# Four first products of two later pairs made ahead from a turned copy of x; the identity made on the chip; the first norm's weights as one row

## The chip, the cores and the metric

The kernel runs on one core of a Trainium2 chip. The metric is the device time of one execution in microseconds (us); of the kernel before there are three runs, and their median counts. A core has five engines, each with a queue of its own: PE (TensorE: matmuls, with the weight loads shown apart as PEld), DVE (VectorE), ACT (ScalarE), POOL (GpSimd) and SP (SyncE, which here issues nearly all DMA transfers). On-chip data lie in SBUF (128 partitions); PE writes to PSUM, eight banks of 128 x 512 floats, of which this kernel uses four with the tag `mm` and four with the tag `acc`.

## The reference

One decoder block on x of 1024 tokens x 1024 features, in float32:

```python
h = x + 0.5 * swiglu(rms_norm(x, ffn1_norm), ffn1_w1, ffn1_w3, ffn1_w2)
u = rms_norm(h, mix_norm)
...                      # u @ w_in, three groups of dilated attention, pooling, gates
h = h + merged @ w_out
h = h + 0.5 * swiglu(rms_norm(h, ffn2_norm), ffn2_w1, ffn2_w3, ffn2_w2)
return rms_norm(h, final_norm)

def rms_norm(x, g):      # per token
    return x * rsqrt(mean(x * x) + 1e-6) * g
def swiglu(x, w1, w3, w2):
    return (silu(x @ w1) * (x @ w3)) @ w2
```

The change touches only the first norm and the first two matrices of the first feed-forward part (D_FF is 2816).

## The kernel before

**Products in three parts.** Every float32 operand is split in a high part (rounded, type f32r) and a low part (the rest). A product of two operands is three matmuls: high x high, high x low, low x high. A *product* here is one of 512 x 512 of x by a 512 x 128 column block of weights, with 4 pieces of 128 along the sum: 12 matmuls of 128 x 128 by 128 x 512.

**Seven products for eight.** x is cut in two halves of features and two of tokens, a weight block in two halves of features and two neighbouring column blocks of 128. With sums and differences of the quarters, seven products give what eight would (Strassen's scheme in Winograd's form). `Quad` holds one such block of `w1` (A) or `w3` (B); `Pair` j (11 of them, `NPAIR`) is the quad A and the quad B of 256 columns. `ORDER = (1, 6, 2, 7, 5, 4, 3)` is the order of the seven products in a quad. Product 1 is x's first quarter `b11` (tokens 0 to 511, features 0 to 511) by the weight's quarter a11; product 2 is `b21` (same tokens, other features) by a12. Products 1 and 2 share one bank, and so do 5 and 3. `Quad.operand(m)` forms the weight side (DVE sums, then `split`: ACT writes the high part, POOL or every third time DVE the rest; four buffers `wc`). `a_out` and `b_out` take the results out of the banks: for product 1, a copy by ACT into `u2` (for A the upper half of the pair's first row y0, for B a tile u); 6 adds to `u2`; product 2's bank, which by then holds 1 + 2, gets its silu (A), or is multiplied into y0 (B).

**The order of work.** Pairs 0 to 2 are begun by `begin_up1` and by `Entry`, whose engine order is written out by hand; `up` finishes them and then runs pairs 3 to 10 one after the other. The results (seven sums a pair) go to DRAM by DMAs on SP; the weights come through `Stream` on SP, into seven buffers of the tag `raw`.

**The start (`begin_up1`).** SP loads the tiles of x (`load_rows`: 128 tokens x 1024 features) and the first weight blocks. For each of the first four tiles ACT squares and sums (`squares`, L274), DVE and POOL make the inverse root (`inverse`), DVE scales the lower 512 features in place by it and by the norm's weights (`scaled_part`, L285), PE turns the result by four transposes against `ident` (`Rows`, L407), ACT writes the high part of the turned tile (L408) and DVE the low part (L411). The first product, `entry.product(0)`, needs all four tiles. PE fills the time before with `keep_on(n)`, n matmuls of ones on ones into a bank `idle` that nobody reads. The norm's weights come as 128 x 8 numbers on ACT's queue, `ident` from DRAM on the same queue; DVE widens the weights to 128 x 1024 (`widen`) and PE turns them into a row that all partitions hold (`gains`). Behind the first product the upper 512 features follow in the same way, with `entry.product(1)` to `(3)` between them.

Of the kernel before, what the change touches and what calls it, by code (L numbers as in the profile page):

```python
# [10 lines left out]
F32 = mybir.dt.float32  # L11
F32R = mybir.dt.float32r
# [125 lines left out]
def tile_block(  # L138
# [46 lines left out]
    def row(name):  # L185
        return keep.tile([P, 1024], F32, tag="raw", bufs=RAW_BUFS, name=name)
# [2 lines left out]
        return keep.tile([P, D], F32, tag="h", bufs=NT, name=name)  # L189


    consts.tile([P, 24], F32, name="pad")
# [79 lines left out]
    def squares(t, out):  # L272
        inv[t] = small.tile([P, 2], F32, tag="nst", name=f"nst_{t}")
        ac.activation(out, h[t], AF.Square, accum_out=inv[t][:, 0:1])  # L274
# [31 lines left out]
    class Sevens:  # L306


        def __init__(self, name, X, fw, fs=None):
            self.name, self.X, self.fw, self.fs = name, X, fw, fs or fw  # L310
            self.n_lo = 0
            self.terms = (0, 1, 2)

        def half_tile(self, tag, n):
            return self.fs.tile([P, HALF], F32, tag=tag, bufs=4, name=f"{tag}_{self.name}{n}")
# [19 lines left out]
    class Quad:  # L335
# [49 lines left out]
        def run(self, m, back=True):  # L385
            if m not in self.w:
                self.operand(m)
            w, n = self.w.pop(m), self.n
            x = {1: "b11", 2: "b21", 3: "b22", 4: "t4", 5: "t1", 6: "t2", 7: "t3"}[m]
            key = {1: "x", 2: "x", 5: "v", 3: "v"}.get(m, m)  # L390
            if m not in (2, 3):
                self.bank[key] = bank("mm" if key in ("x", "v") else "acc", f"u_{self.sv.name}{n}{m}")
            self.sv.product(self.bank[key], w, x, start=m not in (2, 3))
            if m == 3 and back:
                raws.back(2)
            return self.bank[key]
# [140 lines left out]
    class Pair:  # L537
# [48 lines left out]
        def b_out(self, m, p):  # L586
            lows, highs = slice(0, HALF), slice(HALF, S)
            u, j = self.u, self.j
            if m == 1:
                u[2] = self.u2(f"{j}2")  # L590
                ac.activation(u[2], p, AF.Copy)
            elif m == 6:
                ve.tensor_tensor(u[2], p, u[2], op=OP.add)
            elif m == 2:
                c = self.place(0, lows)
                ve.tensor_tensor(c, p, c, op=OP.mult)
            elif m == 7:
                u[3] = self.sv.half_tile("u", f"{j}3")
                ve.tensor_tensor(u[3], p, u[2], op=OP.add)
            elif m == 5:  # L600
                c = self.sv.half_tile("u", f"{j}4")
                ve.tensor_tensor(c, p, u[3], op=OP.add)
                d = self.place(1, highs)
                ve.tensor_tensor(d, d, c, op=OP.mult)
            elif m == 4:
                ve.scalar_tensor_tensor(u[3], p, -1.0, u[3], op0=OP.mult, op1=OP.add)
                d = self.place(1, lows)
                ve.tensor_tensor(d, d, u[3], op=OP.mult)
            else:
                ve.tensor_tensor(u[2], p, u[2], op=OP.add)  # L610
                d = self.place(0, highs)
                ve.tensor_tensor(d, d, u[2], op=OP.mult)
# [31 lines left out]
    def up(sv, sums, between, name, room, begun):  # L644
# [30 lines left out]
            begun[-1].finish()  # L675
        for j in range(len(begun), NPAIR - 1):
            q, then = then or Pair(sv, j, sums), None
            for m in ORDER:
                q.a(m)
            if j == NPAIR - 2:  # L680
                between()
            for m in ORDER[:-2]:
# [5 lines left out]
            for m in ORDER[-2:]:  # L688
                q.b(m)
            q.finish()  # L690
        d = Down(name, sums, sv.half_tile, end)
# [180 lines left out]
    ac.activation(warm, mhalf, AF.Silu)  # L872

    scope = ExitStack()
# [5 lines left out]
    def load_rows(*ts):  # L880
        for t in ts:
            nc.sync.dma_start(h[t], x[t * P:(t + 1) * P, :])

    gain_row = keep.tile([P, D], F32, tag="gain", bufs=1, name="gain_ffn1")
    square = row("square")
    columns_tile = tmp("columns")
    columns = columns_tile.rearrange("p (k c) -> p k c", k=KT)

    def load_all():
        load_rows(0, 1, 2, 3)  # L890
        raws.depth = 2
        raws.load()
        load_rows(4)
        raws.depth = 3
        raws.load()
        load_rows(5)
        raws.depth = 4
        raws.load()
        load_rows(6, 7)
        raws.depth = 6  # L900
        raws.load()
# [5 lines left out]
    def begin_up1():  # L907
# [5 lines left out]
        def keep_on(n):  # L913

            for _ in range(n):
                pe.matmul(idle[:, :P], ones, ones, start=True, stop=True)

        def widen(b):
            k = slice(4 * b, 4 * b + 4)
            ve.tensor_copy(columns[:, k], gain1[:, k, None].to_broadcast([P, 4, P]))  # L920

        def gains(b):

            p = bank("acc", f"gain{b}")
            for k in range(4):
                pe.transpose(p[:, k * P:(k + 1) * P], columns[:, 4 * b + k], ident)
            return p

        r = {}
# [5 lines left out]
        keep_on(12)  # L935
        widen(0)
        squares(0, square)
        widen(1)
        inverse(0)
        g = [gains(b) for b in range(2)]  # L940
        keep_on(2)
        ve.tensor_copy(gain_row[:, LOWS], g[0])
        for t in range(1, 4):
            squares(t, square)
        inverse(1)
        rows(0, "b11", LOWS)
        keep_on(2)
        rows(1, "b11", LOWS)
        inverse(2)
        inverse(3)  # L950
        keep_on(2)
# [4 lines left out]
        rows(2, "b11", LOWS)  # L956
        keep_on(3)
        rows(3, "b11", LOWS, "mm")
        keep_on(2)
        ac.activation(gain_row[:, HIGHS], g[1], AF.Copy)  # L960
        for t in range(4):
            r[t].lower()
        sv1.terms = (0, 2, 1)
# [4 lines left out]
            r[t].keep(h[t][:, LOWS])  # L968

        square2 = columns_tile  # L970
        squares(4, square2)
        for t in (0, 1):
            rows(t, "b21", HIGHS)
        entry.product(1)
        entry.out(0)
        entry.operand(2)
# [2 lines left out]
        r[0].lower()  # L979
        for t in (2, 3):  # L980
            rows(t, "b21", HIGHS)
        for t in (1, 2):
            r[t].lower()
        entry.product(2)
        entry.out(1)
        squares(5, square2)
        r[3].lower()
        for t in range(4):
            r[t].keep(h[t][:, HIGHS])
        entry.product(3)  # L990
# [1357 lines left out]
```

## Time and profile before

| | us |
|---|---|
| median of 3 runs | 1892.95 (1892.79 to 1893.48) |
| the profiled execution | 1892.07 |
| its span in the trace | 1890.2 |
| PE busy | 1879.9 |
| DVE busy | 1331.9 |
| ACT busy | 772.8 |
| POOL busy | 712.2 |

The span is the stretch from the first to the last instruction in the trace; the execution's time holds some 1.9 us around it. All times in the trace count from the span's start. A busy PE is one with a matmul under way; matmuls overlap by about half, so their distance, not their duration, gives the pace.

### The profile page before, as it was taken

To read this page: it belongs to the slowest core of one execution; us is meant where nothing else is said; L and a number is where in the kernel's file an instruction comes from. 1 tells how busy PE (TensorE), PEld (TensorE's weight loads), DVE (VectorE), ACT (ScalarE), POOL (GpSimd) and SP (SyncE) were. 2 spreads that over 40 slices of the span, in tenths; PEclk is the share of its full clock that TensorE was granted. 3 is DMA by queue.
4 is the path that set the end of the run, shared out by engine and by line. 5 is a ranking of instruction groups with operands and counts; after the bars stand their busy time and mean duration, and the time that the engine had idled before them with its cause. 6 is when DMAs were issued, how large, how long until landed. Compare 5 with 4: busy or idle time off the path is not lost.

```text
span 1890.2 us, 24694 instructions
## 1 busy us (share of the span) xinstructions
PE 1879.9 (99%) x8822; PEld 1561.9 (83%) x8822; DVE 1331.9 (70%) x1975; ACT 772.8 (41%) x1394; POOL 712.2 (38%) x533
## 2 busy tenths in 40 slices
PE   9999999999999999999999999999999999999998
PEld 8888888888888888888888888888888888888887
DVE  6776556657786777557885896887665566577867
ACT  7323333333334553334445772363333323334344
POOL 5433333331223254444555357543333333312221
PEclk9999999999999999999999999999999999999999
DMA  5154223436566526765668968744332223454654
GB/s 191 60 198 166 84 89 106 139 111 216 170 224 210 183 84 210 236 219 188 224 236 314 322 224 289 270 153 149 140 127 103 84 102 118 137 189 162 226 197 145
DMA packets 144019, 330.79 MB, mean 175 GB/s; under 512 B 17560, under 2 KB 39064, under 8 KB 142360
## 3 DMA queue, kind: packets, MB, share of 16 engines
q1 hardware_dynamic: 140152, 318.36, 48.6%
q10 hardware_dynamic: 3744, 10.85, 1.6%
q8 instruction: 70, 1.15, 0.3%
q14 instruction: 53, 0.43, 0.1%
HBM read 229.61 MB, written 99.55 MB: 174 GB/s over the span
## 4 chain that ended last, share of the span: by engine, by line
PE 57%; DVE 2%; ACT 1%; DMA 1%; issue 0%; POOL 0%; ACTq 0%; DVEq 0%; SPq 0%
PE u_mixm L331 15%; PE d_f L815 11%; PE wo L2028 4%; PE yp L1770 1%; PE u_f20b L331 1%; PE u_f21a L331 1%; PE u_f210b L331 1%; PE u_f210a L331 1%; PE u_f29b L331 1%; PE u_f29a L331 1%; PE u_f28a L331 1%; PE u_f27b L331 1%; PE u_f27a L331 1%; PE u_f26b L331 1%; PE u_f26a L331 1%; PE u_f25b L331 1%
## 5 line engine op out<-in xcount | busy, mean ns | idle before, releaser
L815 PE MATMUL d_f<-bhi_f,ahi_f 128*128 128x512 f32 x616 | 240.2, 390 | 0.0
L815 PE MATMUL d_f<-bhi_f,alo_f 128*128 128x512 f32 x616 | 239.7, 389 | 0.0
L815 PE MATMUL d_f<-blo_f,ahi_f 128*128 128x512 f32 x616 | 239.6, 389 | 0.0
L772 POOL TENSOR_TENSOR alo_f<-g_f,ahi_f 128x512 fp32r<-128x512 f32 x60 | 85.9, 1448 | 270.0 <-ACT ahi_f L768 270.0
L331 PE MATMUL u_mixm<-xhi_t_mix,wc_mixm 128*128 128x512 f32 x608 | 157.3, 391 | 0.1
L815 PEld LDWEIGHTS d_f<-bhi_f,ahi_f 128*128 128x128 f32 x616 | 115.7, 188 | 24.2 <-ACT h L415 0.5
L815 PEld LDWEIGHTS d_f<-bhi_f,alo_f 128*128 128x128 f32 x616 | 115.6, 188 | 24.2
L815 PEld LDWEIGHTS d_f<-blo_f,ahi_f 128*128 128x128 f32 x616 | 115.7, 188 | 23.7
L331 PEld LDWEIGHTS u_mixm<-xhi_t_mix,wc_mixm 128*128 128x128 f32 x608 | 113.5, 188 | 23.9 <-ACT wc_mixm L319 0.7
L331 PE MATMUL u_mixm<-xhi_b_mix,wc_mixm 128*128 128x512 f32 x456 | 120.4, 391 | 0.0
L322 POOL TENSOR_TENSOR wc_mixm<-s_mixm,wc_mixm 128x512 fp32r<-128x512 f32 x52 | 76.6, 1475 | 104.9 <-ACT wc_mixm L319 94.0
L331 PEld LDWEIGHTS u_mixm<-xhi_b_mix,wc_mixm 128*128 128x128 f32 x456 | 84.9, 188 | 17.3
L319 ACT ACTIVATE wc_mixm<-s_mixm 128x512 fp32r<-128x512 f32 x76 | 47.0, 628 | 109.4 <-DVE s_mixm L373 54.6
L768 ACT ACTIVATE ahi_f<-g_f 128x1024 fp32r<-128x1024 f32 x84 | 81.9, 975 | 3.1 <-DMA g_f<-gs_f 2.0
L331 PE MATMUL u_mixm<-xlo_t_mix,wc_mixm 128*128 128x512 f32 x304 | 81.3, 389 | 0.0
L322 POOL TENSOR_TENSOR wc_mixm<-raw,wc_mixm 128x512 fp32r<-128x512 f32 x40 | 60.2, 1505 | 40.8 <-ACT wc_mixm L319 32.4
L2028 PE MATMUL wo<-w_o,o_hi 128*128 128x512 f32 x224 | 69.3, 390 | 0.0
L768 ACT ACTIVATE bhi_f<-s_f2w 128x512 fp32r<-128x512 f32 x55 | 33.0, 628 | 86.3 <-DVE s_f2w L790 67.6
L768 ACT ACTIVATE bhi_f<-s_f1w 128x512 fp32r<-128x512 f32 x55 | 33.1, 629 | 83.4 <-DVE s_f1w L790 70.2
L331 PEld LDWEIGHTS u_mixm<-xlo_t_mix,wc_mixm 128*128 128x128 f32 x304 | 57.1, 188 | 12.0
L772 DVE TENSOR_TENSOR alo_f<-g_f,ahi_f 128x1024 fp32r<-128x1024 f32 (+1 forms) x48 | 57.6, 1200 | 7.6 <-ACT ahi_f L768 7.5
L331 PE MATMUL u_mixm<-xlo_b_mix,wc_mixm 128*128 128x512 f32 x228 | 61.0, 389 | 0.0
(1332 smaller groups left out, 4751.9 us busy)
## 6 DMA issues: line engine op xcount, KB each, us to landing
g_f<-gs_f SPq DMA_DIRECT2D x70, 512.0 KB
gs_f<-y_f SPq DMA_DIRECT2D x88, 256.0 KB
raw<-in_w2a_dram SPq DMA_DIRECT2D x35, 512.0 KB
raw<-in_w2b_dram SPq DMA_DIRECT2D x35, 512.0 KB
gs_f<-gb_f SPq DMA_DIRECT2D x46, 256.0 KB
raw<-in_w1a_dram SPq DMA_DIRECT2D x22, 512.0 KB
raw<-in_w3a_dram SPq DMA_DIRECT2D x22, 512.0 KB
raw<-in_w1b_dram SPq DMA_DIRECT2D x22, 512.0 KB
```

The costliest lines, as they stand in the source:

```text
L319: ac.activation(w[:, 0], src, AF.Copy)
L322: eng.tensor_tensor(w[:, 1], src, w[:, 0].bitcast(F32), op=OP.subtract)
L331: pe.matmul(p, a, b, start=(start and n == 0), stop=(n == 11), skip_group_check=not start)
L768: ac.activation(hi[:, c], src, AF.Copy)
L772: eng.tensor_tensor(lo[:, d], src[:, o], hi[:, d].bitcast(F32), op=OP.subtract)
L815: pe.matmul(self.banks[m][t], l, r, start=(first and q == 0), stop=(last and q == 2))
L1770: pe.matmul(p, a, b, start=(j == 0), stop=(j == 11))
L2028: pe.matmul(banks[m][t], l, r, start=(st == 0 and j == 0 and q == 0), stop=(st == 1 and j == 1 and q == 2))
```

## The change

1. `ident` is made by POOL (`affine_select` on the tile of ones) and not loaded.
2. The norm's weights come as one row of 1024 on one partition. The row over all partitions is made by two matmuls of a single row of ones by that row (`gains`), and the first 512 weights as columns (`gain1`) by four matmuls of one column each (`gain_columns`) and a copy by ACT. `widen` goes.
3. Ahead of x's tiles SP loads x's first quarter already turned (`x_t`, an input that was there and not read: `led_x`, two blocks of 512 KB) and, among them, the a11 quarter of four weight blocks: of `w1` and `w3` for pairs 4 and 5 (`led_in`, 256 KB each). In `begin_up1` ACT, DVE and POOL scale the turned x by the norm's weights and split it and the four weight quarters; PE makes the four products (`led_run`). The token's inverse root is not in them yet: it is per column of the result, and comes later, as a row (`means`: DVE spreads the four tiles' roots, PE turns them, ACT copies the bank). `led_scaled` multiplies each product by that row on DVE and sends it to DRAM. Two products are first copied out of their banks (`kept`), two stay there.
4. Pairs 4 and 5 leave product 1 out of both quads. Their order is (2, 6, 7, 5, 4, 3). SP fetches the stored products into y0 (before the pair before starts its B) and into u (after the third product of A); product 2's bank now holds 2 alone, and DVE adds the stored part (one addition more in each quad) before the silu or the multiplication.
5. Of the `idle` matmuls, seven at the start remain. The square's scratch lies in a part of X that is not yet used. The pad ahead of `ident` is 16 and not 24 columns wide.

PE before, from the first instruction on, up to the first product `u_f10a1` (`x_b11_t`: the turned tile t; a number after the last underscore is the buffer's):

```order
L916 MATMUL idle_211<-ones_71 128x128 x12
L926 MATMUL gain0_230<-ident_70,columns_143 128x128 x4
L926 MATMUL gain1_235<-ident_70,columns_143 128x128 x4
L916 MATMUL idle_211<-ones_71 128x128 x2
L407 MATMUL x_b11_0_252<-ident_70,x0_133 128x128 x4
L916 MATMUL idle_211<-ones_71 128x128 x2
L407 MATMUL x_b11_1_261<-ident_70,x1_134 128x128 x4
L916 MATMUL idle_211<-ones_71 128x128 x2
L407 MATMUL x_b11_2_277<-ident_70,x2_135 128x128 x4
L916 MATMUL idle_211<-ones_71 128x128 x3
L407 MATMUL x_b11_3_287<-ident_70,x3_136 128x128 x4
L916 MATMUL idle_211<-ones_71 128x128 x2
```

PE now, at the same place, from the end of the second of the four products (`u_led1`) to the first product and the transposes behind it:

```order
L1022 MATMUL u_led1_291<-xhi_t4_f1_118,wc_led1_259 128x512 x4
L409 MATMUL x_b11_0_305<-ident_70,x0_132 128x128 x4
L1022 MATMUL u_led2_315<-xhi_t4_f1_118,wc_led2_281 128x512 x4
L1022 MATMUL u_led2_315<-xlo_t4_f1_119,wc_led2_281 128x512 x4
L1022 MATMUL u_led2_315<-xhi_t4_f1_118,wc_led2_281 128x512 x4
L409 MATMUL x_b11_1_329<-ident_70,x1_133 128x128 x4
L409 MATMUL x_b11_2_339<-ident_70,x2_134 128x128 x4
L1022 MATMUL u_led3_351<-xhi_t4_f1_118,wc_led3_287 128x512 x4
L1022 MATMUL u_led3_351<-xlo_t4_f1_119,wc_led3_287 128x512 x2
L409 MATMUL x_b11_3_359<-ident_70,x3_135 128x128 x4
L1022 MATMUL u_led3_351<-xlo_t4_f1_119,wc_led3_287 128x512 x2
L1022 MATMUL u_led3_351<-xhi_t4_f1_118,wc_led3_287 128x512 x4
```

The four products of 12 matmuls stand where the idle ones stood, with the four tiles' transposes between them; the high parts of x lie in `xhi_t4`, and the weights' in `wc_led`.

POOL before, from its first instruction after the constants (`nst_t`: tile t's inverse root; `wc_f10a1`: the rest of the first product's weights):

```order
L279 TENSOR_TENSOR nst_0_225<-nst_0_225,mhalf_72 128x1
L279 TENSOR_TENSOR nst_1_243<-nst_1_243,mhalf_72 128x1
L279 TENSOR_TENSOR nst_2_245<-nst_2_245,mhalf_72 128x1
L279 TENSOR_TENSOR nst_3_247<-nst_3_247,mhalf_72 128x1
L322 TENSOR_TENSOR wc_f10a1_273<-raw0_195,wc_f10a1_273 128x512
```

POOL now:

```order
L898 AFFINE_SELECT ident_70<-ones_71 128x128
L1009 TENSOR_TENSOR wc_led0_250<-led_w0_142,wc_led0_250 128x512
L1009 TENSOR_TENSOR wc_led1_259<-led_w0_142,wc_led1_259 128x512
L279 TENSOR_TENSOR nst_0_275<-nst_0_275,mhalf_72 128x1
L279 TENSOR_TENSOR nst_1_283<-nst_1_283,mhalf_72 128x1
L1009 TENSOR_TENSOR wc_led2_281<-led_w1_144,wc_led2_281 128x512
L279 TENSOR_TENSOR nst_2_285<-nst_2_285,mhalf_72 128x1
L279 TENSOR_TENSOR nst_3_289<-nst_3_289,mhalf_72 128x1
L1009 TENSOR_TENSOR wc_led3_287<-led_w1_144,wc_led3_287 128x512
L323 TENSOR_TENSOR wc_f10a1_348<-raw0_208,wc_f10a1_348 128x512
```

The four powers now have four operations of 128 x 512 and the select among them, all ahead of the first product's weights.

The diff's core (the lines that allocate, and those that only pass names on, are left out):

```diff
@@ Quad.run, Pair
-            if m not in (2, 3):
+            first = key not in self.bank
+            if first:
                 self.bank[key] = bank("mm" if key in ("x", "v") else "acc", f"u_{self.sv.name}{n}{m}")
...
+            self.led = sv.led.get(j)
+            self.order = ORDER if self.led is None else (2, *(m for m in ORDER if m not in (1, 2)))
...
+        def fetch_a(self):
+            if self.led is not None:
+                nc.sync.dma_start(self.place(0, slice(HALF, S)), self.led[0])
+        def fetch_b(self):
+            if self.led is not None:
+                self.u[2] = self.u2(f"{self.j}2")
+                nc.sync.dma_start(self.u[2], self.led[1])
...
             elif m == 2:
-                ac.activation(self.place(0, lows), p, AF.Silu)
+                c = self.place(0, lows)
+                if self.led is not None:
+                    ve.tensor_tensor(c, p, u2, op=OP.add)
+                    p = c
+                ac.activation(c, p, AF.Silu)
...
@@ the start
-    nc.scalar.dma_start(gain1, ffn1_norm)
-    nc.scalar.dma_start(ident, c_ident)
+    gp.affine_select(out=ident, in_=ones, compare_op=OP.is_equal, fill=0.0, base=0, pattern=[[-1, P]],
+                     channel_multiplier=1)
...
+    nc.scalar.dma_start(columns, ffn1_norm.rearrange("(o p) k -> o (p k)", o=1))
...
     def load_all():
-        load_rows(0, 1, 2, 3)
...
+        features(0)
+        weight(0)
+        features(1)
+        weight(1)
+        load_rows(0)
+        weight(2)
+        load_rows(1, 2)
+        weight(3)
+        load_rows(3)
...
+        def led_low(k):
+            ve.scalar_tensor_tensor(xlo[:, k], led_x[k // 2][:, k % 2], gain1[:, k:k + 1], xhi[:, k].bitcast(F32),
+                                    op0=OP.mult, op1=OP.subtract)
...
+        def led_scaled(q):
+            if q < 2:
+                ve.tensor_tensor(kept[q], kept[q], means, op=OP.mult)
+            else:
+                ve.tensor_tensor(kept[q], led_p[q], means, op=OP.mult)
+            nc.sync.dma_start(led_dram[q], kept[q])
...
+        keep_on(7)
+        gain_columns()
+        g = [gains(b) for b in range(2)]
+        led_high(0)
+        led_high(1, ve)
+        led_split(0)
+        led_rest(0)
+        led_low(0)
+        led_low(1)
+        led_high(2)
+        led_high(3, ve)
+        led_low(2)
+        led_low(3)
+        led_split(1)
+        led_rest(1)
+        led_run(0, by_halves)
         squares(0, square)
+        gain_copy(0)
         inverse(0)
+        ve.tensor_copy(kept[0], led_p[0])
+        led_split(2)
+        squares(1, square)
+        squares(2, square)
+        led_split(3)
+        squares(3, square)
+        led_run(1)
+        rows(0, "b11", LOWS)
         inverse(1)
+        led_rest(2)
+        gain_copy(1)
+        led_run(2)
+        rows(1, "b11", LOWS)
+        inverse(2)
+        ve.tensor_copy(kept[1], led_p[1])
+        rows(2, "b11", LOWS)
+        inverse(3)
+        led_rest(3)
...
         entry.operand(0)
+        led_run(3, by_terms, 0)
+        rows(3, "b11", LOWS)
+        led_run(3, by_terms, 1)
...
         sv1.terms = (0, 2, 1)
         entry.product(0)
```

More of the change, by code (lines that the diff above doesn't have):

```diff
@@ L681, in up @@
                 between()
-            for m in ORDER[:-2]:
+            if j + 1 in sv.led:
+                then = Pair(sv, j + 1, sums)
+                then.fetch_a()
+            for m in q.order[:-2]:
                 q.b(m)
@@ L687, in up @@
                     end.A.operand(m)
-            for m in ORDER[-2:]:
+            for m in q.order[-2:]:
                 q.b(m)
@@ L916, in keep_on, with gain_columns @@
                 pe.matmul(idle[:, :P], ones, ones, start=True, stop=True)
-        def widen(b):
-            k = slice(4 * b, 4 * b + 4)
-            ve.tensor_copy(columns[:, k], gain1[:, k, None].to_broadcast([P, 4, P]))
+        def gain_columns():
+            p = bank("acc", "columns")
+            for k in range(4):
+                pe.matmul(p[:, k:k + 1], columns[:, k], ones[0:1, 0:1], start=True, stop=True)
+            ac.activation(gain1[:, :4], p[:, :4], AF.Copy)
         def gains(b):
             p = bank("acc", f"gain{b}")
-            for k in range(4):
-                pe.transpose(p[:, k * P:(k + 1) * P], columns[:, 4 * b + k], ident)
+            pe.matmul(p.rearrange("m (k p) -> m k p", k=4), ones[0:1, :], columns[:, 4 * b:4 * b + 4],
+                      start=True, stop=True)
             return p
@@ new lines, in begin_up1, with led_run @@
+        by_terms = [(k, i) for i in range(3) for k in range(4)]
+        by_halves = [(k, i) for c in (0, 2) for i in ((0, 1, 2), (0, 2, 1))[c // 2] for k in (c, c + 1)]
+        def led_run(q, order=by_terms, half=None):
+            w = led_w[q]
+            if half != 1:
+                led_p.append(bank("mm", f"u_led{q}"))
+            for n, (k, i) in enumerate(order):
+                if half is None or n // 6 == half:
+                    r = slice(k * P, (k + 1) * P)
+                    a, b = three((w[:, 0, r], w[:, 1, r]), (xhi[:, k, :], xlo[:, k, :]))[i]
+                    pe.matmul(led_p[q], a, b, start=n == 0, stop=n == 11)
@@ L970, in begin_up1 @@
         square2 = columns_tile
+        p = bank("acc", "means")
+        for t in range(4):
+            c = slice(t * P, (t + 1) * P)
+            pe.transpose(p[:, c], spread[:, c], ident)
         squares(4, square2)
@@ L973, in begin_up1 @@
             rows(t, "b21", HIGHS)
+        ac.activation(means, p, AF.Copy)
         entry.product(1)
@@ L981, in begin_up1 @@
             rows(t, "b21", HIGHS)
-        for t in (1, 2):
-            r[t].lower()
+        led_scaled(2)
+        r[1].lower()
+        led_scaled(3)
+        r[2].lower()
         entry.product(2)
@@ L987, in begin_up1 @@
         r[3].lower()
+        for q in (0, 1):
+            led_scaled(q)
         for t in range(4):
```

68 lines of the change are left out of this document (46 added, 22 removed).

## The prediction

> **What bounds the kernel now.** I read the page first, then the waits of PE, then the first 30 us in order of time, because the diff touches the start and two later pairs.
>
> ```profile
> span 1890.2 us, 24694 instructions
> PE 1879.9 (99%) x8822; PEld 1561.9 (83%) x8822; DVE 1331.9 (70%) x1975; ACT 772.8 (41%) x1394; POOL 712.2 (38%) x533
> ```
>
> PE is busy 99% of the span, and its waits in the whole program, longest first, are
>
> ```profile
> PE idle L916 <- DVE mhalf L198: 1.1, 1, 1.1
> PE x_b L407 <- DVE x L285: 0.8, 1, 0.8
> PE o L1711 <- DVE elo L1693: 0.3, 1, 0.3
> ...
> PE u_f10a L331 <- ACT xhi_b_f L408: 0.2, 1, 0.2
> ```
>
> Under 3 us in all, so only two things can shorten the kernel: fewer matmul slots behind the start, or useful work in the slots that now hold `idle` matmuls. The start, in order of time (start, duration, engine, what; in brackets the idle time before it and what ended it):
>
> ```profile
> 0.74 1.81 SPq L882 DMA_DIRECT2D x<-in_x_dram  x4
> ...
> 1.05 4.93 PE L916 MATMUL idle<-ones 128*128 128x128 f32 x24 [1.05 <-DVE mhalf L198]
> ...
> 2.96 0.20 ACT L872 ACTIVATE warm<-mhalf 128x1 f32<-128x1 f32 x1
> ...
> 4.13 1.06 ACT L274 ACTIVATE square<-x 128x1024 f32<-128x1024 f32 x1 [0.97 <-DMA x<-in_x_dram]
> ...
> 4.31 0.76 DVE L920 COPY columns<-gain 128x512 f32<-128x512 f32 x2 [3.31 <-DMA gain<-in_ffn_norm_dram]
> ...
> 5.09 0.19 ACT L274 ACTIVATION_READ_ACCUMULATOR square<-x 128x1 f32 x1
> ...
> 6.55 0.69 DVE L942 COPY gain_ffn<-gain 128x512 f32<-128x512 f32 x1 [1.09 <-PE gain L926]
> ...
> 7.36 1.41 DVE L285 SCALAR_TENSOR_TENSOR x<-x,nst,gain_ffn 128x512 f32<-128x512 f32 x2
> 7.38 0.55 POOL L279 TENSOR_TENSOR nst<-nst,mhalf 128x1 f32<-128x1 f32 x1 [1.28 <-DVE nst L278]
> ...
> 8.66 0.61 PE L916 MATMUL idle<-ones 128*128 128x128 f32 x4
> ...
> 10.29 0.63 ACT L319 ACTIVATE wc_f10a<-raw 128x512 fp32r<-128x512 f32 x1
> ...
> 11.05 0.60 ACT L408 ACTIVATE xhi_b_f<-x_b 128x512 fp32r<-128x512 f32 x1
> ...
> 12.88 2.14 PE L331 MATMUL u_f10a<-xhi_b_f,wc_f10a 128*128 128x512 f32 x8 [0.24 <-ACT xhi_b_f L408]
> ...
> 13.79 2.44 DVE L285 SCALAR_TENSOR_TENSOR x<-x,nst,gain_ffn 128x512 f32<-128x512 f32 x2
> 13.91 1.78 POOL L322 TENSOR_TENSOR wc_f10b<-raw,wc_f10b 128x512 fp32r<-128x512 f32 x1 [1.30 <-ACT wc_f10b L319]
> ...
> 24.63 0.68 ACT L319 ACTIVATE wc_f10a<-raw 128x512 fp32r<-128x512 f32 x1
> ...
> 25.38 1.30 POOL L322 TENSOR_TENSOR wc_f10a<-raw,wc_f10a 128x512 fp32r<-128x512 f32 x1 [3.13 <-ACT wc_f10a L319]
> ...
> 25.70 0.87 PEld L331 LDWEIGHTS u_f10a<-xhi_b_f,wc_f10a 128*128 128x128 f32 x4
> ...
> 28.65 0.60 PE L407 MATMUL x_b<-ident,x 128*128 128x128 f32 x4
> ...
> 29.09 0.60 PE L472 MATMUL x_b<-ident,x 128*128 128x128 f32 x4
> ...
> 29.80 0.70 DVE L466 TENSOR_TENSOR x_b<-x_b,x 128x512 f32<-128x512 f32 x1 [6.15 <-PE x_b L472]
> ```
>
> The first product that counts starts at **12.88 us**; I call this moment T0. What lies before is loading, norms and `idle`; behind it PE has no gap. So the change is worth: the matmul time that it takes out behind T0, less what T0 moves back, less what it adds to PE behind T0.
>
> **The gain: four products.** Pairs 4 and 5 lose product 1 in both of their quads, 4 x 12 matmuls. A pair of today is 14 products:
>
> ```profile
> 173.07 1.07 PE L331 MATMUL u_f14a<-xhi_b_f,wc_f14a 128*128 128x512 f32 x4
> ...
> 211.15 1.07 PE L331 MATMUL u_f15a<-xhi_b_f,wc_f15a 128*128 128x512 f32 x4
> ```
>
> 38.08 us for 14, so 2.72 us a product and 0.227 us a matmul: **-10.88 us**, if PE still sets the pace there. Its neighbours in pair 4 (busy us of PE, PEld, DVE, ACT, POOL):
>
> ```profile
> 172.90:211.00 38.10, 38.10 (x170) 31.55 (x169) 22.78 (x32) 12.22 (x20) 12.49 (x9) 1.00 0.32 109
> ```
>
> The shortened pair lasts 32.6 us. DVE gets two more additions of 0.69 us (as the 0.69 us copy, one bank read), 24.2 us or 74%; ACT and POOL lose work (two copies and two splits of ACT, up to two differences of POOL). DVE stays hidden behind PE; without that cover its additions would cost 1.4 us a pair. The four read-backs on SP (256 KB each) stand between weight loads that are issued a quad ahead; I take 0, and at most 0.5 us for all.
>
> **The cost: T0.** Loads first. SP now issues ten loads before the first weight block, and 2.10 MB stand in front that were not there (two blocks of turned x of 0.52 MB, four half blocks of 0.26 MB). The rate of the queue when full is
>
> ```profile
> 4.00:6.00 2.00, 2.00 (x13) 1.94 (x13) 0.92 (x3) 1.50 (x3) 0.46 (x1) 1.00 1.04 407
> ```
>
> 407 GB/s, and the first 0.52 MB were there at 4.13. So I put the first block of turned x at 4.0, the first weight half at 4.7, the second block at 6.0, x0 at 7.9, x3 at 13.0 and the first weight block at 14.3 us. SP's own 0.45 us an issue (1.81 for four) is done by 5.3, so the bytes decide, not SP. The norm's row comes on ACT's queue in place of 128 short pieces, which landed at 4.31; nothing in this trace shows a single row, so it is between x's first packets (about 2 us) and 4.31. PE needs it at 4.0.
>
> PE's path to the new T0, step by step:
> - Seven `idle` are 14 instructions (twelve were 24). Their early pace, and the shortest, median and longest of 26 of them:
>
> ```profile
> 1.64 1.70 PE L916 MATMUL idle<-ones 128*128 128x128 f32 x7
> ```
>
> ```profile
> L916 PE MATMUL idle<-ones x26: 274/421/582, 1.1 to 6.9; 128*128 128x128 f32 x26
> ```
>
>  Seven in 1.70 us with 0.42 each start (1.70 - 0.42)/6 = 0.21 us apart; the four at 8.66, of 0.27 each, (0.61 - 0.27)/3 = 0.11. So 14 of them end at 1.05 + 14 x 0.21 = 4.0.
> - `gain_columns` is 8 instructions, 0.11 to 0.21 us apart: done at 4.9 to 5.7. ACT's copy (0.20, as `warm`) gives gain1 at 5.3 to 6.1, with a hop of 0.1 either side. The two `gains` are 4 instructions of four times the columns, 0.45 to 0.85 us each: PE is free at 6.7 to 9.1.
> - ACT then makes x's high part and the split of the first weight half (0.63 each): 6.6 to 7.4. POOL's rest takes 1.30 alone and 1.78 beside DVE: 7.9 to 9.2. Here `led_run(0)` really starts to flow; its first four matmuls are done by then.
> - DVE's four `led_low` are two-input operations in SBUF. Alone they take 0.7 (1.41 for two), beside POOL 1.2 (2.44 for two). In the first case the last is done at 9.4 to 10.3 and nobody waits; in the second at about 11.2, and `led_run(0)` waits 0.7 us for it. I take half of that.
> - From there PE has 44 matmuls (10.0 us) and 16 transposes (four of a tile take 0.44, from 28.65 to 29.09, so 1.8 us).
>
> T0 is therefore 19.7 at best, 22.2 at worst, **20.9 us** by the middle: **+8.0 us**.
>
> What runs beside it keeps up: x3 at 13.0, plus square (1.06 and its read 0.19), power 0.55, scaling 0.7 and DVE's queue ahead of them, gives scaled(3) at 17 to 19.2, wanted by PE at 18 to 19.6. POOL's fourth rest and the split of the first weight block end at 19 to 21.4, wanted at about T0 + 0.9. `affine_select` is not in this trace; between a POOL memset and a 128x512 operation it is 0.1 to 1.8 us, and POOL has nothing else until 6.6, nor PE a need of `ident` until 12; cost 0, on either end.
>
> **Behind T0.** Four transposes for the means: +0.45 us on PE. ACT's copy of them (0.60) stands ahead of the split for product 4, which today ends at 25.31 for a PE that begins it at 25.70: 0.4 us spare. PE comes 0.45 later, ACT 0.6 later, but ACT loses the copy of the gain's upper half to DVE; 0 to 0.5, I take 0.2. DVE's eight extra operations (four scalings of 0.69, four spreads of 128 columns, each under the 0.38 of a 512-column copy: 2.8 to 4.3 us) have the 6.15 us of idle before 29.80; were it not there, they would push the scaled rows of tile 4, and PE would wait as long. The bank of product 2 is held by `led_scaled(2)`, about 1 us before PE wants it: 0. SP's four write-outs, 0.45 us each, stand ahead of loads that wait far longer for room: 0. The pad of 16 in place of 24 columns moves addresses only; 0.
>
> **Sum:** +8.0 + 0.45 + 0.2 - 10.88 = **-2.2 us**. The profiled execution took 1892.07 us (span 1890.2 and 1.9 around it), so its like would take 1889.9. The median shown is 0.88 above that execution; against it I forecast **1890.7 us**. With T0 from 19.7 to 22.2 and the waits at their ends (0 to 1.0) the same sum runs from 1889.3 to 1892.9.
>
> **Rivals.**
> *The start is shorter than I count:* columns, split and POOL at their lower ends, no contention, T0 at 19.2 and no waits: -4.1 us, 1888.8. For it: DVE and POOL need not meet. Against it: four handovers in a row, each counted at 0.1.
>
> *The clock comes late.* Today `idle` runs at half pace at first and at full pace by 8.66, and PE had worked without a pause since 1.05. With seven `idle` and then matmuls on a single row, PE pauses until the split is there, and the full pace may come a stretch later, so that 6 to 12 matmuls of `led_run` go at twice 0.227: +1.4 to +2.7, T0 near 22.4, 1892.2. The Trainium skill says it so (TensorE: Matmul & The Clock Gate, Part 1): the gate looks at a window of about 3.4 us that runs freely, and gives the full clock after a busy one; the two paces of `idle` in this trace agree. By that rule the moment also differs from execution to execution.
>
> *The four products do not come back.* Place: the quads of pairs 4 and 5. If what PE waits for there is a chain through DVE (the sum of the kept part, then the place of the second row, which is free only when the pair before has been sent off) and no longer its own matmuls, the quads keep their 19.0 us, and all that T0 lost stays: +8.6, 1901.6. It decides from the point where that chain is over 16.3 us a quad; by the busy times DVE is at 12.1 of these. A return of under 5 us, of 10.88, makes the kernel slower by more than 0.2%.
>
> *The change doesn't do what it says:* the products are not made in free slots but behind loads, x3 and its scaling set T0, at 23 or more: -0.1, 1892.9. Against it: 1 to 2 us in hand at x3.
>
> **Chances.** Forecast 0.59, short start 0.12, late clock 0.14, no return 0.09, loads 0.06. A measurement of this kernel can tell about 0.2% (3.8 us) from no change, so faster is below 1889.2: the short start and a sliver of the forecast, 0.13. Slower is above 1896.7: only the products that don't come back, 0.08. Within: 0.79. The range from 1888.3 to 1894.2 takes in forecast, short start, late clock and loads, with an upper end for a small part of the return lost.
>
> **What would show it.** In the changed profile: `led_run` in PE's rows from about 7 us, dense from about 9; the first u_f10a at 20.9 (19.7 to 22.2); ten to twelve us between `led_run(0)`'s last part and T0; no wait of PE over 0.5 us behind it; pairs 4 and 5 of 32.6 us each. Wrong if T0 is beyond 23, if a gap stands before product 2 or at tile 4's transposes, or if the u_f14 and u_f15 quads last over 16.5 us.

## The result, and the profile after

The changed kernel takes **1915.26 us** (median of 4 runs, 1914.26 to 1915.64), the one before 1893.22 in the same session: ratio 1.0116, 95% interval [1.0098, 1.0133], **22.0 us slower**. The profiled execution took 1915.05 us, with a span of 1913.3.

The page of the changed kernel begins:

```profile
span 1913.3 us, 24698 instructions
PE 1903.8 (100%) x8798; PEld 1561.7 (82%) x8798; DVE 1347.3 (70%) x1993; ACT 773.4 (40%) x1393; POOL 709.7 (37%) x535
```

PE has fewer instructions than before (8798, 8822 before) and is busy 23.9 us longer. So the time did not go into waits. The waits of PE in the changed kernel, longest first, say the same:

```profile
PE idle L967 <- DVE mhalf L198: 1.1, 1, 1.1
PE o L1840 <- DVE elo L1822: 0.3, 1, 0.3
PE u_mixm L332 <- ACT wc_mixm L320: 0.3, 1, 0.3
```

When the bound engine waits no more than before and is busy longer with less to do, its instructions have become longer. The groups of PE by line and tile show which. First of the kernel before, then of the changed one (behind the first bar: busy us and mean ns of one; behind the second: idle us just before):

```profile
L815 PE MATMUL d_f<-bhi_f,ahi_f 128*128 128x512 f32 x616 | 240.2, 390 | 0.0
L331 PE MATMUL u_mixm<-xhi_t_mix,wc_mixm 128*128 128x512 f32 x608 | 157.3, 391 | 0.1
...
L331 PE MATMUL u_f13a<-xhi_t_f,wc_f13a 128*128 128x512 f32 x32 | 8.2, 389 | 0.0
...
L331 PE MATMUL u_f25a<-xhi_t_f,wc_f25a 128*128 128x512 f32 x32 | 8.2, 389 | 0.0
```

```profile
L843 PE MATMUL d_f<-bhi_f,ahi_f 128*128 128x512 f32 x616 | 240.2, 390 | 0.1
L332 PE MATMUL u_mixm<-xhi_t_mix,wc_mixm 128*128 128x512 f32 x608 | 161.0, 397 | 0.3 <-ACT wc_mixm L320 0.3
...
L332 PE MATMUL u_f13a<-xhi_t_f,wc_f13a 128*128 128x512 f32 x32 | 8.4, 396 | 0.0
...
L332 PE MATMUL u_f25a<-xhi_t_f,wc_f25a 128*128 128x512 f32 x32 | 8.2, 389 | 0.0
```

One line of code, one shape, two answers: the products of the first feed-forward block (f1) and of the mixer (`u_mixm`) take 396 and 397 ns where they took 389 and 391, those of the second block (f2) are as before. So are the down products (`d_f`, on another line). These durations overlap with those of the neighbours. What counts is the time from one start to the next, which I worked out from the trace for every pair of neighbours within a product (mean of the middle 80%): f1 and mixer 226.7 ns before and **233.4** after, f2 226.7 in both.

The start of the changed kernel, in order of time:

```profile
1.10 3.26 PE L967 MATMUL idle<-ones 128*128 128x128 f32 x14 [1.10 <-DVE mhalf L198]
4.30 2.06 PE L972 MATMUL columns<-ones,columns 1*128 1x1 f32 x8
6.22 3.89 PE L978 MATMUL gain<-columns,ones 1*128 1x512 f32 x4
10.04 1.22 PE L1022 MATMUL u_led<-xhi_t_f,wc_led 128*128 128x512 f32 x2
11.06 1.05 PE L1022 MATMUL u_led<-xlo_t_f,wc_led 128*128 128x512 f32 x2
11.91 2.69 PE L1022 MATMUL u_led<-xhi_t_f,wc_led 128*128 128x512 f32 x6
...
25.05 2.03 PE L332 MATMUL u_f10a<-xhi_b_f,wc_f10a 128*128 128x512 f32 x8
```

T0, the start of the first u_f10a, is **25.05 us** (12.88 before, 20.9 forecast). The stretches of the start (length, busy time of PE, PEld, DVE, ACT, POOL, then the granted clock, DMA share and GB/s) tell a part of why:

```profile
6.00:8.00 2.00, 2.00 (x4) 0.69 (x5) 1.13 (x2) 1.48 (x4) 0.08 (x1) 0.89 1.00 382
8.00:10.00 2.00, 2.00 (x3) 0.30 (x1) 2.00 (x3) 1.36 (x3) 1.93 (x2) 0.50 0.95 339
10.00:12.00 2.00, 2.00 (x6) 1.57 (x6) 2.00 (x3) 1.58 (x3) 0.92 (x1) 0.50 0.99 394
12.00:14.00 2.00, 2.00 (x6) 1.57 (x5) 1.19 (x3) 1.55 (x3) 0.56 (x1) 0.50 1.04 422
14.00:16.00 2.00, 2.00 (x9) 1.61 (x8) 0.89 (x2) 1.73 (x4) 0.00 (x0) 0.90 1.02 414
```

The clock was granted at 4.1 us, withdrawn at 7.6 and back at 14.4; from 10.0 to 14.4 the products made ahead ran at half pace (six in 2.69 us). Before, it was granted at 5.2 and stayed.

The four products did come back. The same tile's matmuls in pairs 3 and 6 (times of the first and the last start), before and after:

```profile
L331 PE MATMUL u_f13a<-xhi_b_f,wc_f13a x24: 389/389/389, 135.0 to 153.8; 128*128 128x512 f32 x24
```

```profile
L331 PE MATMUL u_f16a<-xhi_b_f,wc_f16a x24: 389/389/389, 249.2 to 268.0; 128*128 128x512 f32 x24
```

```profile
L332 PE MATMUL u_f13a<-xhi_b_f,wc_f13a x24: 395/396/396, 150.1 to 169.5; 128*128 128x512 f32 x24
```

```profile
L332 PE MATMUL u_f16a<-xhi_b_f,wc_f16a x24: 395/396/396, 256.5 to 275.9; 128*128 128x512 f32 x24
```

From pair 3 to pair 6 it was 114.2 us and is 106.4: 7.8 us shorter, which is 10.9 for 48 matmuls less, and 456 others at 6.7 ns more (3.1).

So the lag behind the kernel before is 12.2 at T0, 15.1 at pair 3, 7.3 at pair 6, 12.9 where the down products of the first block begin (452.5 for 439.6), 22.7 at the mixer's last products, and 22.8 at the end. Sum: +12.2 (T0), -10.9 (four products), +11.6 (pace in f1), +9.9 (from the mixer on, nearly all of it pace).

### The profile page after: what moved, and what is told of

Same layout as the page of the kernel before. It is cut to its first block, busy times and chain, and to the rows that moved or that the text cites. A ratio compares the mean times of both kernels' runs of the same rounds, so it can differ in the third digit from the quotient of the medians.

```text
span 1913.3 us, 24698 instructions
## 1 busy us (share of the span) xinstructions
PE 1903.8 (100%) x8798; PEld 1561.7 (82%) x8798; DVE 1347.3 (70%) x1993; ACT 773.4 (40%) x1393; POOL 709.7 (37%) x535
## 4 chain that ended last, share of the span: by engine, by line
PE 54%; DVE 3%; ACT 2%; issue 1%; DMA 1%; POOL 1%; ACTq 0%; SPq 0%; DVEq 0%; POOLq 0%
PE u_mixm L332 15%; PE d_f L843 8%; PE wo L2157 4%; PE yp L1899 1%; PE u_f20b L332 1%; PE u_f21a L332 1%; PE u_f210b L332 1%; PE u_f210a L332 1%; PE u_f29b L332 1%; PE u_f29a L332 1%; PE u_f28b L332 1%; PE u_f28a L332 1%; PE u_f27b L332 1%; PE u_f27a L332 1%; PE u_f26b L332 1%
```

## Experiments: what made the matmuls slower

My theory came from one line of the change that touches no instruction: the pad of 16 in place of 24 columns. All tiles of the left-hand pool behind it, X among them, lie 32 bytes lower; the split weights of f1 and mixer lie in the right-hand pool and don't move with it. In f2 both operands are in the left-hand pool, and so they are in the down products. In bytes of a partition, as the built program has them, for the first product: its tile of X (the moving operand, the 128x512 piece in PE's row) lies at 36064 before and 36032 after, its split weight (the stationary operand, the 128x128 piece that PEld loads) at 118752 and 135136. The weight's shift, 16384 bytes, comes from elsewhere in the change (it is there with the pad put back too) and is a multiple of 256; it will turn out not to count. **Put back the pad**, in the changed kernel:

```diff
-    consts.tile([P, 16], F32, name="pad")
+    consts.tile([P, 24], F32, name="pad")
```

> The changed kernel with the pad of 24 columns put back, nothing else. Theory (phase): in the changed kernel the moving operand X lies at 0 and the weight halves at 32 modulo 64 bytes in 3396 of the ffn1 and mixer matmuls, and each is 6.7 ns later for it; with the pad of 24 both lie at 32 again. Then four product matmuls take 0.907 us again in place of 0.932, and the time is 1915.3 - 3396 x 0.0067 = 1892.5 us, between 1891.5 and 1894.5 (the later start, +12.2, against the four products saved, -10.9, is all that is left). Rival (the edit's other parts): the pace comes from the new code, the start flags, the extra transfers or the longer program; then the pace stays at 0.932 and the time at 1915 +- 1.

Measured: 1894.66 us, ratio to the kernel before 1.0011 [1.0003, 1.002]; of the 22.0 us over the kernel before 2.0 are left (0.2 over the upper end of my range; T0 was 25.68 in its profile, 0.6 later than I had taken it). The groups:

```profile
L332 PE MATMUL u_mixm<-xhi_t_mix,wc_mixm 128*128 128x512 f32 x608 | 157.3, 391 | 0.7 <-ACT wc_mixm L320 0.7
...
L332 PE MATMUL u_f13a<-xhi_t_f,wc_f13a 128*128 128x512 f32 x32 | 8.2, 389 | 0.0
```

226.7 ns again from start to start. **The pad alone, in the kernel before:**

```diff
-    consts.tile([P, 24], F32, name="pad")
+    consts.tile([P, 16], F32, name="pad")
```

> The kernel before with the pad cut from 24 to 16 columns, nothing else. Theory (phase): 3444 matmuls get operands at 0 and 32 modulo 64, so 1893.2 + 3444 x 0.0067 = 1916.3 us, between 1914 and 1918, and four product matmuls of ffn1 take 0.932 us; ffn2's products, which get 0 and 0, keep 0.907. Rival (the edit's other parts): 1893.2 +- 1 and 0.907 everywhere.

Measured: 1914.5 us, ratio 1.0115 [1.0101, 1.0129]:

```profile
L331 PE MATMUL u_mixm<-xhi_t_mix,wc_mixm 128*128 128x512 f32 x608 | 161.0, 397 | 0.0
...
L331 PE MATMUL u_f13a<-xhi_t_f,wc_f13a 128*128 128x512 f32 x32 | 8.4, 396 | 0.0
...
L331 PE MATMUL u_f25a<-xhi_t_f,wc_f25a 128*128 128x512 f32 x32 | 8.2, 389 | 0.0
```

With not one instruction other than before, the kernel is as slow as the changed one. Eight columns of padding are the cause, shown from both sides. Is it where X lies, or how X and weights lie to each other? **The right-hand pool moved too**, in the changed kernel, pad 16:

```diff
+    keep.tile([P, 8], F32, name="pad_right")
```

> The changed kernel with its pad of 16 as it is, and 8 columns (32 bytes) more at the outer end of the right-hand pool, so that the weight halves move to 0 modulo 64 too. Theory (phase: what counts is that the two operands differ): both at 0, fast again, 1892.5 us (1891.5 to 1894.5). First rival (what counts is that the moving operand lies at 0): still slow, 1915 +- 1. Second rival (the edit's other parts): 1915 +- 1.

Measured: 1895.0 us, ratio 1.0012 [1.0003, 1.0021], 226.7 ns: fast again, if 0.5 us over my range. **The right-hand pool alone**, the same line in the kernel before:

> The kernel before with 8 columns (32 bytes) more at the outer end of the right-hand pool: the weight halves of 3444 matmuls of ffn1 and mixer move to 0 modulo 64, X stays at 32. Theory (phase: any difference counts): 1916 us (1914 to 1918). Rival (only a moving operand at 0 beside weights at 32 is slow): 1893.2 +- 1. Rival (the edit's other parts): 1893.2 +- 1.

Measured: 1914.28 us, ratio 1.0115 [1.0101, 1.0128], 233.4 ns. It is the distance of the two operands, not the place of either. What distance is good? I had put it modulo 64, since 0 and 32 were all that I had seen. **X moved inside its space** tries that: the tiles of X become 16 columns longer and begin 4 columns (f1) or 1 column (f2) later, so that their distances to the weights differ from tile to tile.

```diff
-            s: tuple(pool.tile([P, 4, HALF], F32R, ...) for part in ("hi", "lo"))
+            s: tuple(pool.tile([P, 4 * HALF + 16], F32R, ...)[:, o:o + 4 * HALF] ...
-    consts.tile([P, 32], F32, name="pad2")
```

> The kernel before with the tiles of X moved inside their space: those of ffn1 to 48 modulo 64 and those of ffn2 to 36 modulo 64, against weights at 32 in both (pad2, 128 bytes, left out to make room). Theory A (any difference modulo 64 costs 6.7 ns a matmul): 2 x 1848 matmuls, 1892.6 + 24.8 = 1917 us. Theory B (only the 32-byte half of the 64 counts; 36, 48 and 32 lie in one): 1892.6 +- 1, pace 0.907 for four in both. Theory C (a difference of 16 counts, one of 4 does not, or the other way about): 1905.

Measured: 1935.62 us, ratio 1.0226 [1.0213, 1.024], slower than any of my three theories:

```profile
L337 PE MATMUL u_mixm<-xhi_t_mix,wc_mixm 128*128 128x512 f32 x608 | 160.7, 396 | 0.0
...
L337 PE MATMUL u_f25a<-xhi_t_f,wc_f25a 128*128 128x512 f32 x32 | 8.6, 399 | 0.0
...
L337 PE MATMUL u_f13a<-xhi_t_f,wc_f13a 128*128 128x512 f32 x32 | 8.4, 394 | 0.0
```

The first row refutes modulo 64: I had left the mixer's products alone, but leaving out pad2 moved their X by 128 bytes, and they slowed to 232.5 ns. Over all kernels only distances of 0 and 256 bytes modulo 512 had run at 226.7. Two runs with other pads in the kernel before settle it, **64 bytes further**:

```diff
-    consts.tile([P, 24], F32, name="pad")
+    consts.tile([P, 40], F32, name="pad")
```

> The kernel before with the pad of 40 columns: X 64 bytes further, so that moving and stationary operand of 3444 matmuls differ by 64 modulo 256 (modulo 64 they agree). Theory A (what counts is the difference modulo 256, as the run with X at 16 and 4 bytes suggests, where the mixer's pair at a difference of 128 took 232.5 ns in place of 226.7): 4 to 6.7 ns a matmul, 1892.7 + 14 to 23 = 1907 to 1916 us. Theory B (modulo 64, as first put): 1892.7 +- 1.

Measured: 1900.36 us, ratio 1.0041 [1.0027, 1.0055]; 229.0 ns, and 3444 times 2.3 ns are the 7.9 us, near the 7.6 measured. Less than theory A's range, but not theory B's zero:

```profile
L331 PE MATMUL u_mixm<-xhi_t_mix,wc_mixm 128*128 128x512 f32 x608 | 158.7, 393 | 0.1
```

And **256 bytes further**, a pad of 88 columns:

> The kernel before with the pad of 88 columns: X 256 bytes further, a difference of 0 modulo 256. Theory A (modulo 256): 1892.7 +- 1, pace 226.7 ns. Rival (any pad but 24 is slow, or modulo 512 counts): 1907 to 1916 us.

Measured: 1892.45 us, ratio 0.9998 [0.9989, 1.0007], 226.7 ns. The pace by the distance from stationary to moving operand, modulo 256 bytes, from start to start of 128x512 products of two fp32r operands:

| distance | 0 | 16 | 32 | 64 | 80 | 128 | 144 | 208 | 224 | 4, 68, 132, 196 |
|---|---|---|---|---|---|---|---|---|---|---|
| ns | 226.7 | 230.8 | 233.4 | 229.0 | 231.7 | 232.5 | 233.0 | 234.9 | 233.4 | 236.3 to 238.4 |

0 is from the kernel before and the last run, 32, 64 and 224 each from a run above, the others from the run with X moved; these depend by up to about 1 ns on which of two neighbours' distances a gap is put down to. Of the distances tried, only 0 modulo 256 runs at 226.7. Why that is so was not tried and stays open.

## Experiments: what made the start longer

With the pad put back the kernel is still 2.0 us slower than before, with T0 at 25.68. The forecast had -2.2. **More idle products ahead**, so that the clock is granted first (on the pad of 24, as all that follow):

```diff
-        keep_on(7)
+        keep_on(12)
```

> The changed kernel with the pad of 24 and with twelve idle products (24 matmuls) ahead of the norm's columns, as before, in place of seven. Theory (clock): with seven, the full clock comes at about 14.5 us, so the gains and the first eight matmuls of the products made ahead run at half pace; with twelve it comes at about 5.3 as in the kernel before. The idle ones then end at 6.1, columns and gains at full pace at about 9.2, the 44 matmuls and 16 transposes follow in 11.8, and the first u_f10a starts at 21.0 to 22.0 in place of 25.7; time 1894.7 - 3.9 = 1890.8 us (1890 to 1892). Rival (data): squares, scaled rows and POOL set the start of u_f10a; it stays at 24 to 25.7 with waits of PE in between, 1893.5 to 1895. Second rival: matmuls on one row don't hold the clock, which is withdrawn after a stretch; then 1892.5 to 1894.

Measured: 1896.08 us, ratio 1.0016 [1.0008, 1.0025], T0 25.43 (in the profiled execution, the fastest of eleven, 1894.43): no gain, and a median above what any of the three had given. The granted clock in this kernel:

```profile
6.00:8.00 2.00, 2.00 (x7) 1.62 (x8) 0.37 (x1) 0.54 (x2) 0.00 (x0) 0.85 1.03 409
8.00:10.00 2.00, 2.00 (x3) 0.61 (x2) 1.73 (x3) 2.00 (x5) 1.05 (x1) 0.50 1.02 356
10.00:12.00 2.00, 2.00 (x4) 0.83 (x3) 2.00 (x2) 1.86 (x5) 1.95 (x2) 0.50 1.01 397
12.00:14.00 2.00, 2.00 (x6) 1.51 (x5) 2.00 (x4) 1.84 (x4) 0.00 (x0) 0.50 1.05 426
```

The clock came and was withdrawn again, as the second rival said, though at a higher price than it had. PE was "busy" throughout by these rows, but from 5.3 to 11 us with matmuls on one row. **Without the gains on PE**, again with twelve idle products, the row spread by a DMA of 0.5 MB instead:

```diff
...
+            nc.sync.dma_start(spread_gain, ffn1_norm.rearrange("(o p) k -> o (p k)", o=1).to_broadcast([P, D]))
...
+        keep_on(12)
         gain_columns()
-        g = [gains(b) for b in range(2)]
```

> As the run with twelve idle products, and the norm's row spread over the partitions by a DMA (0.5 MB, ahead of x0 on SP's queue) in place of the two gains matmuls on PE; DVE copies it out with a stride. Theory (clock and PE's own work): 2 us less on PE ahead of the products made ahead, the first u_f10a at 19.5 to 20.5; 1889 to 1890.5 us. Rival (loads): the 0.5 MB put x0 to x3 1.3 us later, and the scaled rows set the start: 1890.5 to 1892. Rival (weights): PE waits from about 7 us until POOL and DVE have made the first low parts at 9 to 10, so that nothing is gained: 1891.

Measured: 1894.61 us, ratio 1.0009 [1.0, 1.0018], T0 26.28. This one is a miss for the theory as I put it, and for both rivals: the columns products on one row and a gap of 1.5 us behind them were enough for the clock to go again (3.41 us granted, then 6.83 not). It tells nothing on the gains themselves. **The row form alone**, in the kernel before, with the identity made on the chip and nothing made ahead:

```diff
-    nc.scalar.dma_start(gain1, ffn1_norm)
-    nc.scalar.dma_start(ident, c_ident)
+    gp.affine_select(out=ident, in_=ones, compare_op=OP.is_equal, fill=0.0, ...)
...
-                pe.transpose(p[:, k * P:(k + 1) * P], columns[:, 4 * b + k], ident)
+            pe.matmul(p.rearrange("m (k p) -> m k p", k=4), ones[0:1, :], columns[:, 4 * b:4 * b + 4],
+                      start=True, stop=True)
...
-        widen(0)
...
-        widen(1)
```

> The kernel before with the identity made on the chip and the norm's weights as one row with two products on one row for the gain row, and nothing made ahead. Theory (clock): the full clock is withdrawn for a stretch after the one-row products; the first u_f10a comes 0 to 3 us later than 12.9 and its first matmuls may run at half pace: 1893 to 1896 us. Rival (this part is neutral, only the work made ahead costs): 1892 to 1893, the clock granted once and kept.

Measured: 1897.1 us, ratio 1.0021 [1.0012, 1.0031], 4.4 us more than before, all of it ahead of T0 (17.33 for 12.88):

```profile
6.01 3.91 PE L923 MATMUL gain<-columns,ones 1*128 1x512 f32 x4
9.85 1.23 PE L918 MATMUL idle<-ones 128*128 128x128 f32 x4
...
15.13 1.08 PE L918 MATMUL idle<-ones 128*128 128x128 f32 x6
...
17.33 2.11 PE L331 MATMUL u_f10a<-xhi_b_f,wc_f10a 128*128 128x512 f32 x8 [0.24 <-ACT xhi_b_f L408]
```

Before, the idle ones behind the gains:

```profile
6.78 0.61 PE L916 MATMUL idle<-ones 128*128 128x128 f32 x4
```

Four idle ones in 1.23 us are half pace (0.61 before). So a part of the change that makes nothing ahead costs 4.4 us by itself, more than the 0 to 3 that I had put. 3.1 us of it are the gains' own length (9.85 for 6.78); 1.4 came in what follows, which runs at half pace until 15.6. **The columns as before**, with the products made ahead, closes the ring: the norm in 128 pieces, widened by DVE, eight transposes, and idle products until the weights are split.

```diff
...
-        keep_on(7)
-        gain_columns()
-        g = [gains(b) for b in range(2)]
+        keep_on(12)
+        widen(0)
+        widen(1)
         led_high(0)
         led_high(1, ve)
+        g = [gains(b) for b in range(2)]
+        keep_on(8)
```

> The changed kernel with the pad of 24, twelve idle products, and the gain row made as in the kernel before (norm in 128 pieces, widened by DVE, eight transposes of 128x128) in place of the products on one row; eight more idle products until the first weights are split. Theory (clock): in the runs with one-row products the full clock is withdrawn for 6.83 us, because PE is hardly busy in them; with transposes and idle products it is granted at about 5.3 us and stays. The products made ahead then begin at 8.5 to 9.5 at full pace and the first u_f10a starts at 20.5 to 22 in place of 25.7: 1894.7 - 4.3 = 1890.4 us (1889.5 to 1892). Rival (weights and loads set the start): PE waits between the products made ahead, first u_f10a at 24 or later, 1893 to 1895.

Measured: **1891.74 us**, ratio to the kernel before 0.9995 [0.9986, 1.0004], T0 22.01:

```profile
6.38 1.22 PE L976 MATMUL gain<-ident,columns 128*128 128x128 f32 x8
7.44 1.95 PE L966 MATMUL idle<-ones 128*128 128x128 f32 x16
9.14 0.71 PE L1019 MATMUL u_led<-xhi_t_f,wc_led 128*128 128x512 f32 x2
...
22.01 1.97 PE L332 MATMUL u_f10a<-xhi_b_f,wc_f10a 128*128 128x512 f32 x8
```

The clock was granted once, at 6.7 us, and kept. This is the best version seen: 2.9 us under the changed kernel with its pad put back. Against the kernel before, its interval reaches over 1, so that it can't be told from it. Last, **the four products made but not used** (pairs 4 and 5 make all fourteen):

```diff
-            sv1.led.setdefault(LED[q // 2], [None, None])[q % 2] = led_dram[q]
```

> The changed kernel with the pad of 24; the four products are made, scaled and stored as in the change, but pairs 4 and 5 don't read them and make all fourteen products. Theory (the four products come back in full): 48 matmuls of 0.227 us more than the pad-24 kernel, 1894.7 + 10.9 = 1905.6 us (1905 to 1906.5), first u_f10a at 25 to 26 as there. Rival (they don't come back): 1895 to 1901.

Measured: 1904.84 us, ratio 1.0064 [1.005, 1.0077], 10.2 us over the kernel that uses them (0.2 under my range). The products come back. The 0.7 us missing to 10.9 I put to the start, which differs from one execution to the next with the moment of the clock: in the profiled one T0 was 24.45, 1.2 us earlier than with the products used.

## Why the prediction was wrong, point by point

*What bounds the kernel: right.* PE without waits, before and after. I drew from it that only fewer slots or a later T0 can change the time, and took the length of a slot, 0.227 us, for a constant. That was the hidden premise.

*"The pad of 16 in place of 24 columns moves addresses only; 0": this step failed.* It cost 20.0 us (22.0 over the kernel before, and 2.0 with the pad put back), nearly the whole difference. It moves 3396 matmuls of f1 and mixer from 226.7 to 233.4 ns. At 6.7 ns each that is 22.8 us, and 20.7 came: 11.6 in f1 and 9.1 from the mixer on, since 0.8 of the 9.9 is there with the pad put back too. Why not all of it shows was not tried. None of my rivals had it, nor the range. The trace before could not show the price; but the one row that every term rests on, 0.227 us, was open to whatever the change moved, and zero was put down without a row on either side.

*The gain of the four products, -10.88: right.* 114.2 us between pairs 3 and 6 became 106.4, which is -10.9 with the new pace taken off. The run with the pad put back shows it without that: 103.4 us, 10.8 less.

```profile
L332 PE MATMUL u_f13a<-xhi_b_f,wc_f13a x24: 389/389/389, 147.8 to 166.6; 128*128 128x512 f32 x24
```

```profile
L332 PE MATMUL u_f16a<-xhi_b_f,wc_f16a x24: 389/389/389, 251.2 to 270.0; 128*128 128x512 f32 x24
```

The run that leaves them unused gives 10.2. My sign of error, quads over 16.5 us, did show, since a quad of 72 matmuls at 233.4 ns is 16.8; but it was the pace and not the chain through DVE, and the rival of no return is refuted.

*T0, +8.0 forecast, +12.2 measured: too small, outside its own range (22.2).* Behind the first four matmuls of the products made ahead I had PE flow from 9.1 (20.9 less the 11.8 of PE's work); the fifth began at 11.91, and from there to T0 it took 13.1 us. (The terms as written, 9.2, 0.7 and 11.8, give 21.7 for the worst case, not 22.2.) Three things failed. `gain_columns` was put at 0.9 to 1.7 us and took 1.9 (4.30 to 6.22). The `gains` were put at 0.45 to 0.85 us for each of four instructions, by four times the columns of an `idle`; they took 0.97 (3.89 for four), in the full clock and in the half one alike. And the late clock, which I gave 0.14, is what happened, at the price that I gave it: ten matmuls of the products made ahead begin at half pace (10.04 to 14.05), where I had 6 to 12. The Trainium skill has the clock rise after a busy window of some 3.4 us and fall after an idle one (TensorE: Matmul & The Clock Gate, Part 1); the traces agree in the stretch, 3.41 us granted and then twice that without. But PE, by its rows, was not idle then. So the rival's number came by another mechanism: I had feared the clock for a wait of PE behind the one-row matmuls, and there was none; the clock went while those matmuls ran, as it did in the run of the row form alone. What in them doesn't hold the clock, the single row or their slow stream, was not separated.

*Behind T0, +0.45 and +0.2; DVE's extra operations, SP's issues, `affine_select`: right within what can be seen.* The waits of PE are 0.3 us at the most; with the pad put back, the kernel's lag falls from 12.8 at T0 to 2.0 at pair 6. From T0 to pair 3, where the 0.65 should show, the lag grows by less than 0.1 us there and by 0.45 in the run with the columns as before. The operation that the trace before lacked:

```profile
1.12 0.29 POOL L898 TENSOR_SCALAR_AFFINE_SELECT ident<-ones 128x128 f32<-128x128 f32 x1 [0.63 <-DVE mhalf L198]
```

(from the run with the pad put back): 0.29 us, at the lower end of 0.1 to 1.8. Loads came later than I put them (x0's square begins at 9.87 us in the changed kernel, where I had the landing at 7.9), but PE waited for none of them.

*The sum without the pad.* -2.2 was forecast, +2.0 measured; with the columns as before and the clock held, -1.0, which can't be told from 0. What was left of my sum was T0: 22.0 in place of 20.9 even then.

## What to carry over

When a change moves nothing but addresses, compare where the operands of the bound engine's matmuls lie to each other before writing down 0: here, of the distances tried, only those with the stationary and the moving operand equal modulo 256 bytes ran at the full pace, and 32 bytes of difference cost 3% of every product. When the bound engine waits no more than before and is busy longer with fewer instructions, look for a group whose mean duration moved, and then for the groups of the same line and shape that did not move; what sets them apart names the cause. At this kernel's start, the clock went in every trace with the matmuls on one row in which it had come by then, and stayed where full-size transposes and idle matmuls stood in their place: count such small things at their own length, and look at what they do to the clock.

## What the runs showed of the hardware that I had not expected

- The pace of 128x512 products of fp32r operands depends on the distance of their operands in a partition: 226.7 ns at 0 modulo 256 bytes, 229.0 to 234.9 at the other multiples of 16 that were tried, 236.3 to 238.4 at 4 beyond a multiple of 64. Moving both by the same 32 bytes left the pace at 226.7.
- Not every group follows that rule. Those of the products made ahead that stand right behind transposes or idle matmuls ran at about 230 ns with a distance of 0 (others of them at 226.7), and the `yp` products of the mixer, between attention's small matmuls, had a median duration of 394 to 395 ns in every kernel, at any distance. The reason was not looked for.
- fp32 matmuls on one row with 512 columns took 0.92 to 1.06 us from start to start, at half and at full clock.
- The granted clock's row reads 1.00 until the first record of the clock: in the kernel with the pad put back it shows 1.00 from the start, though six products took 2.76 us at 12.1. The matmuls' own pace is the surer sign.
